# Splitting four elementwise operations of a decoder step into halves: the rotation's multiplication and addition, the low parts of rotated tiles, and the scaling of paired weights

## Chip, cores and metric

The kernel runs on one core of one Trainium2 chip. The metric is the device time of one launch in microseconds; below 3466.3 us stands as the median of three runs of the kernel before (3462.27 to 3474.13). The engines are called as the profile calls them: PE is TensorE, DVE is VectorE, ACT is ScalarE, POOL is GpSimd, SP is SyncE, which here issues all DMAs.

## The reference

One step of a two-layer decoder trunk: a pooling layer, then an attention layer with three dilated groups that share one K/V, for 2048 prompt rows and 8 sample rows of width 1024, all in fp32. What the change touches lies in the projections to q, k and v and in the rotation of q and k:

```python
def rope_partial(x, pos):                     # the first 16 of 64 dims of each head
    half = ROT_DIM // 2
    inv = 1.0 / (ROPE_THETA ** (jnp.arange(0, ROT_DIM, 2, dtype=jnp.float32) / ROT_DIM))
    ang = pos.astype(jnp.float32)[:, None] * inv[None, :]
    cos, sin = jnp.cos(ang)[None, :, None, :], jnp.sin(ang)[None, :, None, :]
    x1, x2 = xr[..., :half], xr[..., half:]
    rot = jnp.concatenate([x1 * cos - x2 * sin, x1 * sin + x2 * cos], axis=-1)
...
kv = (rmsnorm(h, g) @ w_kv).reshape(B, T, N_GROUPS, 2, HEADS_PER_GROUP, HEAD_DIM)
q  = (rmsnorm(h, g) @ w_in)[..., :N_GROUPS * ATTN_WIDTH]      # the rest is the gate
...
y_prompt = rmsnorm(h_p + attn_out(outs_p, gate_p, w_b_out[j]), g_final)
```

The gain `g` of the norm is folded into the weights by the kernel: each weight tile is multiplied by it before use. That is the scaling which the change splits.

## The kernel before, in words

Everything is transposed: 128 features lie on the partitions, tokens along the free axis. Each fp32 matrix is split into a high part (a copy by ACT into the type fp32r) and a low part (the rest, one subtraction), and each product is three matmuls: high by high, high by low, low by high.

The stages, with the time at which each begins in the profiled execution:

1. Pooling layer, from 0 us, in four quarters of 512 tokens.
2. Gates of half 0 (tokens 0 to 1023), from about 657 us.
3. **The paired stage**, from about 757 to 1660 us: q, k and v of half 0. A `Pair` takes the weights of two heads' blocks together (9 for each of 4 head pairs, 36 in all) and makes seven products of half the depth instead of eight (`run_pair`). Its two raw weights of 128x1024 are loaded into `wst` or, for every second pair, `pairh`; `Pair.scale` multiplies each by the gain (`w_scale`, L127, on POOL); `s1` and `s3` (L196, L199, POOL) and `s2` and `s4` (L202, L205, DVE) form sums and differences; `hi` (L212, ACT) and `lo` (L215, DVE) split the seven operands into `ringh` and `ringl`, which PE reads. The results are put together in `raw` (or `pairl`) by ACT copies (L921) and DVE additions (L924).
4. Half 1 (tokens 1024 to 2047), from about 1640 to 3210 us: one weight at a time (`Unit`, whose scaling stays one operation), and beside it, from about 1790 us, the prompt's attention (`prompt_attn`), one step a tick.
5. The output product and the last norm, from about 3220 us.

Rotation (`Rope`): when both heads of a unit are complete, their 16 rotated rows are gathered into one tile `xs` by DMAs (`gather`), three ticks later `turn` multiplies `xs` by the table `cs2` (L790, 128x1024; on DVE in half 0, on POOL in half 1) and adds the lower 64 partitions to the upper 64 (L791, always DVE). DMAs put the rows back into `raw` (L794). Then `split` makes the high part `rh` (L811, ACT) and, two ticks later, `low` subtracts it (L815: DVE in half 0, POOL in half 1) and stores both.

A tick is one `yield` of the dense products, after 8 matmuls or so. `plan` sets at which tick of a product the next weights are loaded, scaled and split; `defer(n, f)` runs f n ticks later. This gives the order in which instructions are written; a scheduler of the framework then fixes the order on each engine's own queue, and from there on each engine works strictly in order. The sample rows' attention (`sample_attn`) runs as a side job in the paired stage, with its products on POOL (L1038, L1070) and its sums on DVE (L1041, L1072).

Of the kernel before, what the change touches and what calls it, by code (L numbers as in the profile page):

```python
# [12 lines left out]
F32 = mybir.dt.float32  # L13
F32R = mybir.dt.float32r
AF = mybir.ActivationFunctionType
OP = mybir.AluOpType
AX = mybir.AxisListType

P = 128
# [4 lines left out]
HALF = 1024  # L24
TOT = SEQ + NB
NQ = 4
QN = SEQ // NQ
# [3 lines left out]
DIL = (1, 4, 16)  # L31
# [22 lines left out]
def step_kernel(ctx: ExitStack, tc: tile.TileContext, a: dict):  # L54
    nc = tc.nc
    vec, act, pool, pe = nc.vector, nc.scalar, nc.gpsimd, nc.tensor
    load_dma = store_dma = nc.sync.dma_start
# [37 lines left out]
    N = type("N", (), {})()  # L95
    N.w1 = rpool

    KH2 = KT // 2
# [27 lines left out]
    def w_scale(st, gs):  # L126
        pool.tensor_tensor(st, st, gs[:, :, None].to_broadcast([P, KT, P]), OP.mult)  # L127
# [19 lines left out]
    class Unit:  # L147
# [9 lines left out]
        def scale(self):  # L157
            if self.gs is not None:
                w_scale(self.st, self.gs)
# [13 lines left out]
    class Pair:  # L173
# [15 lines left out]
                      for i_ in range(2) for j in range(2)}  # L189

        def scale(self, i):
            w_scale(self.st[i], self.gs[i])

        def s1(self):
            self.t = N.bt.tile([P, KH2, P], F32, name="ws1")
# [98 lines left out]
    def defer(ticks, fn):  # L294
        deferred.append([ticks, fn])
# [430 lines left out]
    def perm(ap, g):  # L726

        return ap.rearrange("p (l r) -> p r l", r=DIL[g])

    def permd(ap, g):  # L730
        return ap.rearrange("p (r l) -> p r l", r=DIL[g])
# [36 lines left out]
    class Rope:  # L768
# [18 lines left out]

        def turn(self):
            xs, g, eng = self.xs, self.g, (vec, pool)[self.hf]
            eng.tensor_tensor(permd(xs, g), permd(xs, g), perm(N.cs2, g), OP.mult)  # L790
            vec.tensor_add(xs[0:64], xs[0:64], xs[64:128])  # L791
            for u, (kind, p, raw) in enumerate(self.units):
                for b in range(2):
                    load_dma(raw[64 * b:64 * b + 16], xs[32 * u + 16 * b:32 * u + 16 * b + 16])  # L794
                defer(3 + 2 * u, lambda kind=kind, p=p, raw=raw: self.split(kind, p, raw))

        def dst(self, kind, p, x):
            v = qkd[kind][self.g][p].rearrange("h d x n -> (h d) x n")[:, x]
# [2 lines left out]
        def split(self, kind, p, raw):  # L801
            g = self.g
            if kind == 1:
                if g == 2:
                    store_dma(a["o_k2"][self.hf, p], raw)
                elif self.hf == 1 and g == 0:
                    store_dma(a["o_k0"][p], raw[:, HALF - P:])
                elif self.hf == 1:
                    store_dma(a["o_k1"][p], permd(raw, g)[:, :, P:])
            rh = N.bw.tile([P, HALF], F32R, name="rh", bufs=1)  # L810
            act.activation(rh, raw, AF.Copy)  # L811
            store_dma(self.dst(kind, p, 0), permd(rh.bitcast(F32), g))

            def low():
                (vec, pool)[self.hf].tensor_sub(raw.bitcast(F32R), raw, rh.bitcast(F32))  # L815
                store_dma(self.dst(kind, p, 1), permd(raw, g))
                if self.hf == 1:
                    done[p, g] = done.get((p, g), 0) + 1
            defer(2, low)
# [800 lines left out]
```

## Time and profile before

| | before |
|---|---|
| median of three runs | 3466.3 us (3462.27 to 3474.13) |
| profiled execution, its own time | 3453.65 us |
| span of its instructions | 3451.6 us |
| PE busy | 3187.5 us (92%) |
| DVE busy | 2000.7 us (58%) |
| ACT busy | 1715.3 us (50%) |
| POOL busy | 1680.1 us (49%) |
| mean granted TensorE clock | 0.969 of full speed |

Busy times of engines overlap. PE is busy nearly all the time, so what can be won or lost by the other engines is bounded by how often PE stands still: a look at the waits of PE, stage by stage, comes before a look at what any single instruction takes.

### The profile page before, as it was taken

What the parts mean: (1) busy time and instruction counts of PE and PEld (TensorE: products, weight loads), DVE (VectorE), ACT (ScalarE), POOL (GpSimd) and SP (SyncE); (2) the same over time, 40 slices, a digit from 0 to 9 for tenths busy, and PEclk for the clock granted to TensorE, in tenths of its full rate; (3) what the DMA queues carried; (4) which work ended last, traced back from release to release, by engine and by line L of the source; (5) the groups of instructions that cost most, each with busy time, mean ns of one, the idle gap of its engine ahead of it and who ended that gap; (6) DMA issues with size and microseconds to landing.
All of it is one profiled execution on the core that took longest, in us unless ns stands there. A gap on an engine that the chain in (4) does not pass through costs nothing.

```text
span 3451.6 us, 56978 instructions
## 1 busy us (share of the span) xinstructions
PE 3187.5 (92%) x19608; PEld 2799.4 (81%) x19608; DVE 2000.7 (58%) x3989; ACT 1715.3 (50%) x3812; POOL 1680.1 (49%) x1026
## 2 busy tenths in 40 slices
PE   8999899899998998987989999999999999999798
PEld 8887678699887887877778877888787888887698
DVE  6745665526767667676426555656464646564345
ACT  3333433324434443334227766776666676778221
POOL 5566765624234354343454454545454645552342
PEclk9999999999999999999999999999999999999899
DMA  4434443434576766767777767687777777774653
GB/s 135 145 129 159 141 156 110 129 98 135 154 185 209 177 193 180 201 198 201 195 206 205 194 187 187 189 201 196 181 194 181 198 182 194 196 199 131 192 155 120
DMA packets 547744, 596.96 MB, mean 173 GB/s; under 512 B 216904, under 2 KB 407752, under 8 KB 547448
## 3 DMA queue, kind: packets, MB, share of 16 engines
q1 hardware_dynamic: 547456, 593.32, 61.7%
q8 instruction: 156, 2.56, 0.3%
q14 instruction: 132, 1.08, 0.1%
HBM read 371.77 MB, written 184.04 MB: 161 GB/s over the span
## 4 chain that ended last, share of the span: by engine, by line
PE 32%; DMA 11%; DVE 5%; ACT 4%; SPq 3%; issue 3%; POOL 2%; DVEq 0%; POOLq 0%; ACTq 0%
PE psd L241 20%; PE pss L1211 3%; PE ppt L1232 3%; PE ppo L1276 1%; PE ppo L1278 1%; DMA spb<-pd 1%; DMA statd<-st 1%; ACT pr L1224 1%; DMA vr<-vd 1%; DMA raw<-xs 1%; DMA qt<-qd 1%; DMA wst<-in_wKV 1%; PE ppo L1273 1%; DVE xs L791 1%; DMA cyt<-yd 1%
## 5 line engine op out<-in xcount | busy, mean ns | idle before, releaser
L1163 POOL CAST qt<-qt 64x1024 fp32r<-64x1024 f32 x192 | 207.1, 1079 | 435.1 <-DMA qt<-qd 371.9
L1224 ACT ACTIVATE pr<-pr,st 128x256 f32<-128x256 f32 (+1 forms) x768 | 345.9, 453 | 126.0 <-DVE st L1218 124.7
L1218 DVE CUSTOM_DVE_ANT_0 pr<-pss,mask 128x256 f32<-128x256 f32 (+1 forms) x768 | 248.5, 360 | 175.7 <-PE pss L1211 118.5
L1248 DVE TENSOR_TENSOR pl<-ppt,ph 128x512 fp32r<-128x512 f32 (+2 forms) x384 | 216.1, 570 | 190.0 <-ACT ph L1244 187.2
L168 POOL TENSOR_TENSOR ringl<-wst,ringh 128x1024 fp32r<-128x1024 f32 x96 | 241.6, 2519 | 124.0 <-ACT ringh L163 72.5
L1211 PE MATMUL pss<-kt,qt 128*128 128x256 f32 (+1 forms) x1536 | 261.2, 288 | 12.8 <-DVE st L1218 7.8
L127 POOL TENSOR_TENSOR wst<-wst,gvec 128x1024 f32<-128x1024 f32 x88 | 177.3, 2017 | 184.8 <-DMA wst<-in_wKV 99.1
L241 PE MATMUL psd<-hn_2h,ringh 128*128 128x512 f32 x640 | 259.2, 405 | 6.6 <-ACT raw L837 5.0
L241 PE MATMUL psd<-hn_3h,ringh 128*128 128x512 f32 x640 | 260.9, 408 | 4.1 <-ACT hn_3h L643 2.4
L163 ACT ACTIVATE ringh<-wst 128x1024 fp32r<-128x1024 f32 x184 | 193.3, 1052 | 139.2 <-PE psd L241 94.9
L241 PE MATMUL psd<-hn_2l,ringh 128*128 128x512 f32 x640 | 257.2, 402 | 5.1 <-DVE hn_2l L644 5.1
L241 PE MATMUL psd<-hn_3l,ringh 128*128 128x512 f32 x640 | 259.4, 405 | 2.5 <-DVE hn_3l L644 2.5
L241 PE MATMUL psd<-hn_2h,ringl 128*128 128x512 f32 x640 | 258.7, 404 | 0.0
L241 PE MATMUL psd<-hn_3h,ringl 128*128 128x512 f32 x640 | 258.4, 404 | 0.0
L1211 PEld LDWEIGHTS pss<-kt,qt 128*128 128x128 f32 x1536 | 223.2, 194 | 29.4 <-DVE st L1218 8.7
L1232 PE MATMUL ppt<-ident,pr 128*128 128x128 f32 x1200 | 209.6, 281 | 36.0 <-DVE pl L1248 23.0
L1244 ACT ACTIVATE ph<-ppt 128x512 fp32r<-128x512 f32 (+2 forms) x384 | 189.7, 500 | 91.6 <-PE ppt L1232 87.1
L168 DVE TENSOR_TENSOR ringl<-wst,ringh 128x512 fp32r<-128x512 f32 x176 | 148.4, 878 | 139.5 <-ACT ringh L163 139.3
L970 PE MATMUL pwx<-t1h,ringh 128*128 128x256 f32 (+1 forms) x576 | 171.1, 297 | 26.4 <-DVE pairl L924 14.0
L1232 PEld LDWEIGHTS ppt<-ident,pr 128*128 128x128 f32 x1200 | 143.1, 142 | 63.1 <-issue 22.5
L1190 POOL TENSOR_TENSOR vt<-vr,vt 128x512 fp32r<-128x512 f32 (+1 forms) x96 | 136.4, 1421 | 80.8 <-ACT vt L1189 72.4
L1276 PE MATMUL ppo<-ph,vt 128*128 128x128 f32 (+1 forms) x688 | 167.6, 274 | 7.6 <-ACT ph L1244 5.7
(301 smaller groups left out, 9828.3 us busy)
## 6 DMA issues: line engine op xcount, KB each, us to landing
qt<-qd SPq DMA_DIRECT2D x192, 256.0 KB
wst<-in_wKV SPq DMA_DIRECT2D x72, 512.0 KB
kt<-kd SPq DMA_DIRECT2D x288, 128.0 KB
wst<-in_wA SPq DMA_DIRECT2D x64, 512.0 KB
wst<-in_wQ SPq DMA_DIRECT2D x52, 512.0 KB
kd<-rh SPq DMA_DIRECT2D x48, 512.0 KB
qd<-rh SPq DMA_DIRECT2D x48, 512.0 KB
vd<-vt SPq DMA_DIRECT2D x96, 256.0 KB
```

Source lines behind the costliest of these rows:

```text
L127: pool.tensor_tensor(st, st, gs[:, :, None].to_broadcast([P, KT, P]), OP.mult)
L163: act.activation(self.w[0], self.st, AF.Copy)
L168: self.eng.tensor_sub(self.w[1][:, k], self.st[:, k], self.w[0][:, k].bitcast(F32))
L241: pe.matmul(ps[:, :n], u[:, k, ws], v[:, k, c0:c1], start=(k, i) == order[0], stop=(k, i) == order[-1])
L1163: pool.tensor_copy(qr[64:128], qr[0:64])
L1211: pe.matmul(ps[:, sl], qt[:, x, qc], kt_[:, kc], start=x == 0, stop=x == 1)
L1218: vec.tensor_tensor_reduce(pr[:, lo:], ps[:, sl], mask[:, lo:], 1.0, BIG, OP.add, OP.min, st[:, 0, h, col:col + 1])
L1224: act.activation(pr[:, lo:], pr[:, lo:], AF.Exp, bias=st[:, 0, h, col:col + 1], scale=-1.0, accum_out=st[:, 1, h, col:col + 1])
L1232: pe.transpose(pt[:, (2 * bb + x) * P:(2 * bb + x + 1) * P], pr[:, x * P:(x + 1) * P], ident)
L1244: act.activation(PB[i][0][:, s], pv[:, s], AF.Copy)
L1248: vec.tensor_sub(PB[i][1][:, s], pv[:, s], PB[i][0][:, s].bitcast(F32))
L1276: pe.matmul(po[:, q0:q1], vt[:, kb + 1, h].rearrange("p x d -> p (x d)"), xh, start=first, stop=False, skip_group_check=True)
```

## The change

- `Pair.scale`: 72 multiplications of 128x1024 on POOL become 144 of 128x512.
- `Rope.turn`: the multiplication and the addition are done for one half of the columns, and one tick later (`defer(1, rest)`) for the other; the DMAs back to `raw` and the splits follow that second part. 24 multiplications on DVE, 24 on POOL and 48 additions on DVE become twice as many of half the size.
- `Rope.split`, `low`: in half 0 the 48 subtractions on DVE are done in two halves, the second a tick later, and the store of the low part waits for both. In half 1 nothing changes here.

```diff
--- before.py
+++ after.py
@@ -189,7 +189,10 @@
         def scale(self, i):
-            w_scale(self.st[i], self.gs[i])
+            for j in range(2):
+                k = slice(j * KH2, j * KH2 + KH2)
+                pool.tensor_tensor(self.st[i][:, k], self.st[i][:, k],
+                                   self.gs[i][:, k, None].to_broadcast([P, KH2, P]), OP.mult)
@@ -787,12 +790,22 @@
         def turn(self):
             xs, g, eng = self.xs, self.g, (vec, pool)[self.hf]
-            eng.tensor_tensor(permd(xs, g), permd(xs, g), perm(N.cs2, g), OP.mult)
-            vec.tensor_add(xs[0:64], xs[0:64], xs[64:128])
-            for u, (kind, p, raw) in enumerate(self.units):
-                for b in range(2):
-                    load_dma(raw[64 * b:64 * b + 16], xs[32 * u + 16 * b:32 * u + 16 * b + 16])
-                defer(3 + 2 * u, lambda kind=kind, p=p, raw=raw: self.split(kind, p, raw))
+            lh = HALF // DIL[g] // 2
+
+            def part(i):
+                c = slice(lh * i, lh * i + lh)
+                x = permd(xs, g)[:, :, c]
+                eng.tensor_tensor(x, x, perm(N.cs2, g)[:, :, c], OP.mult)
+                vec.tensor_add(x[0:64], x[0:64], x[64:128])
+            part(0)
+
+            def rest():
+                part(1)
+                for u, (kind, p, raw) in enumerate(self.units):
+                    for b in range(2):
+                        load_dma(raw[64 * b:64 * b + 16], xs[32 * u + 16 * b:32 * u + 16 * b + 16])
+                    defer(3 + 2 * u, lambda kind=kind, p=p, raw=raw: self.split(kind, p, raw))
+            defer(1, rest)
@@ -812,7 +825,18 @@
             def low():
-                (vec, pool)[self.hf].tensor_sub(raw.bitcast(F32R), raw, rh.bitcast(F32))
+                if self.hf == 1:
+                    pool.tensor_sub(raw.bitcast(F32R), raw, rh.bitcast(F32))
+                    fin()
+                else:
+                    lo_part(0)
+                    defer(1, lambda: (lo_part(1), fin()))
+
+            def lo_part(i):
+                c = slice(QN * i, QN * i + QN)
+                vec.tensor_sub(raw[:, c].bitcast(F32R), raw[:, c], rh[:, c].bitcast(F32))
+
+            def fin():
                 store_dma(self.dst(kind, p, 1), permd(raw, g))
```

The queues of the engines stand as follows where the prediction speaks of them. Lines of the changed kernel are its own: L798 and L799 are L790 and L791 of before, L218 is L215, L948 is L924, L205 is L202, L1065 is L1041, L837 is L815 in half 0, L194 is L127 for pairs.

DVE, in the paired stage, at the fourth rotation of the third head pairs (the burst at 1319 us of the profile). Before:

```order
L215 TENSOR_TENSOR ringl<-pairh,ringh 128x512
L790 TENSOR_TENSOR xs<-xs,cs_5539 128x1024
L215 TENSOR_TENSOR ringl<-pairh,ringh 128x512
L791 TENSOR_TENSOR xs<-xs 64x1024
L215 TENSOR_TENSOR ringl<-wst,ringh 128x512
L924 TENSOR_TENSOR pairl<-pairl,pwx 128x256
L202 TENSOR_TENSOR wst<-ws_11746,wst 128x512
L1041 TENSOR_REDUCE sg_t_11720<-skt 35x16
```

The same place in the changed kernel:

```order
L218 TENSOR_TENSOR ringl<-pairh,ringh 128x512
L798 TENSOR_TENSOR xs<-xs,cs_5539 128x4x128 x2
L218 TENSOR_TENSOR ringl<-pairh,ringh 128x512
L799 TENSOR_TENSOR xs<-xs 64x4x128 x2
L218 TENSOR_TENSOR ringl<-wst,ringh 128x512
L948 TENSOR_TENSOR pairl<-pairl,pwx 128x256
L205 TENSOR_TENSOR wst<-ws_11857,wst 128x512
L1065 TENSOR_REDUCE sg_t_11831<-skt 35x16
```

The halves stand where the whole operations stood, both of a kind in a row; nothing else has come between them.

SP, at the end of the attention: the last stores of the merged attention (`yd`, L1366, now L1390) and the first load of an output weight (`in_wB`). Before:

```order
L765 DMA sgd_85<-sgb 128x1024
L1366 DMA yd_93<-ot_31351 128x512
L1499 DMA ch_33346<-h1d_70 128x288
L1458 DMA cyt<-yd_86 128x296
L1366 DMA yd_93<-ot_31600 128x512
L1460 DMA cgt<-sgd_78 128x296
L1499 DMA ch_33346<-h1d_71 128x288
L1458 DMA cyt<-yd_87 128x296
L1458 DMA cyt<-yd_86 128x288
L1460 DMA cgt<-sgd_78 128x288
L123 DMA wst<-in_wB 128x1024
```

In the changed kernel, from the last of these stores but one:

```order
L1390 DMA yd_93<-ot_31586 128x512
L1523 DMA ch_33562<-h1d_71 128x288
L1482 DMA cyt<-yd_87 128x296
L1484 DMA cgt<-sgd_79 128x296
L1523 DMA ch_33562<-h1d_72 128x288
L1390 DMA yd_93<-ot_31826 128x512
L1484 DMA cgt<-sgd_80 128x296
L1482 DMA cyt<-yd_88 128x296
L1523 DMA ch_33562<-h1d_73 128x288
L1482 DMA cyt<-yd_86 128x288
L1484 DMA cgt<-sgd_78 128x288
L123 DMA wst<-in_wB 128x1024
```

Between the last store and the weight there are five DMAs in both; between the last two stores there are now four instead of two.

PE, just ahead of the output product (L1359, now L1383, spreads the merge's weights; the rows with `cy0h` are the first of the output product). Before:

```order
L241 MATMUL psd<-hn_3h,ringl 128x512
L1359 MATMUL pws<-spread_15549,sel 128x512
L241 MATMUL psd<-hn_3h,ringh 128x512
L241 MATMUL psd<-hn_3l,ringh 128x512
L1359 MATMUL pws<-spread_15550,sel 128x512
L241 MATMUL psd<-hn_3h,ringl 128x512
L1359 MATMUL pws<-spread_15550,sel 128x512 x2
L241 MATMUL psd<-cy0h,wbh_33101 128x288
```

In the changed kernel:

```order
L244 MATMUL psd<-hn_3h,ringh 128x512
L244 MATMUL psd<-hn_3l,ringh 128x512
L244 MATMUL psd<-hn_3h,ringl 128x512
L1383 MATMUL pws<-spread_15723,sel 128x512 x3
L1383 MATMUL pws<-spread_15724,sel 128x512 x3
L244 MATMUL psd<-cy0h,wbh_33326 128x288
```

Six of the merge's matmuls now come after the last dense one, where there were two.

## Rows read from the trace of the kernel before

**Rows 1.** The profile's page: span, and busy time of three engines with its share of the span and the number of instructions.
```profile
span 3451.6 us, 56978 instructions
PE 3187.5 (92%) x19608; PEld 2799.4 (81%) x19608; DVE 2000.7 (58%) x3989; ACT 1715.3 (50%) x3812; POOL 1680.1 (49%) x1026
```

**Rows 2.** Busy time of the engines in the paired stage, in half 1 with the attention, and from its end on: stretch, its length, then each engine with its instructions, the granted TensorE clock, the share of DMA engines, GB/s.
```profile
757.00:1660.00 903.00, 813.47 (x5545) 747.41 (x5544) 619.46 (x749) 362.42 (x703) 364.45 (x194) 0.96 0.66 182
1660.00:3180.00 1520.00, 1442.22 (x8831) 1238.38 (x8830) 823.95 (x2415) 1007.08 (x2570) 772.02 (x504) 0.98 0.72 191
3180.00:3452.00 272.00, 232.06 (x1538) 218.67 (x1536) 125.40 (x277) 67.51 (x142) 86.33 (x98) 0.92 0.50 151
```

**Rows 3.** Waits of PE in the paired stage, from 757 to 1660 us: who waited for what, us in total, times, the longest.
```profile
PE pwx L970 <- DVE ringl L215: 22.0, 6, 6.6
PE pwx L970 <- DVE pairl L924: 14.0, 8, 3.2
PE pwx L970 <- DVE raw L924: 10.7, 9, 2.0
PE pwy L970 <- DVE ringl L215: 6.7, 6, 3.2
```

**Rows 4.** Groups of instructions in the paired stage by line and shape, DVE first, then POOL: busy us, mean ns of one, idle time of the engine before them and what ended it.
```profile
L215 DVE TENSOR_TENSOR ringl<-wst,ringh 128x512 fp32r<-128x512 f32 x108 | 104.7, 974 | 40.7 <-ACT ringh L212 20.8 <-PE psd L241 18.5
L215 DVE TENSOR_TENSOR ringl<-pairh,ringh 128x512 fp32r<-128x512 f32 x108 | 101.5, 946 | 20.2 <-ACT ringh L212 18.4
L791 DVE TENSOR_TENSOR xs<-xs 64x1024 f32<-64x1024 f32 x24 | 49.3, 2056 | 0.8
```
```profile
L127 POOL TENSOR_TENSOR wst<-wst,gvec 128x1024 f32<-128x1024 f32 x25 | 54.9, 2201 | 58.5 <-DMA wst<-in_wKV 27.7 <-DVE ringl L215 20.3 <-DVE xs L790 6.3
L127 POOL TENSOR_TENSOR pairh<-pairh,gvec 128x1024 f32<-128x1024 f32 x24 | 51.0, 2138 | 72.1 <-DMA pairh<-in_wKV 64.8 <-DVE ringl L215 7.3
...
L127 POOL TENSOR_TENSOR wst<-wst,gq 128x1024 f32<-128x1024 f32 x13 | 27.0, 2077 | 49.3 <-DVE xs L790 24.5 <-DMA wst<-in_wQ 22.9 <-DVE ringl L215 1.9
...
L127 POOL TENSOR_TENSOR pairh<-pairh,gq 128x1024 f32<-128x1024 f32 x12 | 25.0, 2083 | 64.6 <-DMA pairh<-in_wQ 62.0 <-DVE ringl L215 2.6
```

**Rows 5.** Single durations by line, min/median/max in ns, with the first and the last start in us; the first three in the paired stage, the last two over the whole span.
```profile
L215 DVE TENSOR_TENSOR ringl<-wst,ringh x108: 671/692/2841, 759.3 to 1591.3; 128x512 fp32r<-128x512 f32 x108
```
```profile
L127 POOL TENSOR_TENSOR wst<-wst,gq x13: 1887/1898/2641, 825.0 to 1595.8; 128x1024 f32<-128x1024 f32 x13
```
```profile
L196 POOL TENSOR_TENSOR ws<-wst x18: 1267/1290/1622, 756.3 to 1554.9; 128x512 f32<-128x512 f32 x18
```
```profile
L815 POOL TENSOR_TENSOR raw<-raw,rh x45: 2359/2392/2737, 1687.9 to 3076.8; 128x1024 fp32r<-128x1024 f32 x45
L815 DVE TENSOR_TENSOR raw<-raw,rh x24: 1203/1220/2744, 807.6 to 1657.5; 128x1024 fp32r<-128x1024 f32 x24
```

**Rows 6.** Timeline of the burst at 1319 us: start, duration, engine, line; in brackets the idle time before it and what ended it. DVE, then POOL, then PE.
```profile
1319.12 2.01 DVE L790 TENSOR_TENSOR xs<-xs,cs 128x1024 f32<-128x1024 f32 x1 [2.93 <-DMA sqb<-tokd]
...
1321.76 5.13 DVE L791 TENSOR_TENSOR xs<-xs 64x1024 f32<-64x1024 f32 x1
1327.03 2.17 DVE L215 TENSOR_TENSOR ringl<-wst,ringh 128x512 fp32r<-128x512 f32 x1
```
```profile
1321.07 2.89 POOL L1038 TENSOR_TENSOR skt<-skt,sqb 35x1024 f32<-35x1024 f32 x1 [6.76 <-DMA sqb<-tokd]
1323.92 1.88 POOL L127 TENSOR_TENSOR pairh<-pairh,gq 128x1024 f32<-128x1024 f32 x1
1325.98 2.67 POOL L127 TENSOR_TENSOR pairh<-pairh,gq 128x1024 f32<-128x1024 f32 x1 [0.17 <-DMA pairh<-in_wQ]
```
```profile
1329.25 0.58 PE L970 MATMUL pwx<-hn_0h,ringl 128*128 128x256 f32 x1 [6.62 <-DVE ringl L215]
```

**Rows 7.** Timeline of the burst at 1592 us: DVE, then POOL.
```profile
1592.05 2.92 DVE L791 TENSOR_TENSOR xs<-xs 64x1024 f32<-64x1024 f32 x1
1595.10 0.69 DVE L215 TENSOR_TENSOR ringl<-pairh,ringh 128x512 fp32r<-128x512 f32 x1
```
```profile
1591.99 1.90 POOL L127 TENSOR_TENSOR wst<-wst,gvec 128x1024 f32<-128x1024 f32 x1 [4.01 <-DMA wst<-in_wKV]
```

**Rows 8.** Half 1: the additions of the rotation as a group (1660 to 3180 us), one of them in the timeline, and what POOL does around it; and PE's longest total wait there.
```profile
L791 DVE TENSOR_TENSOR xs<-xs 64x1024 f32<-64x1024 f32 x24 | 47.1, 1961 | 35.7 <-POOL xs L790 21.6 <-DMA qt<-qd 6.1 <-DMA spb<-pd 5.8
```
```profile
2105.43 2.91 DVE L791 TENSOR_TENSOR xs<-xs 64x1024 f32<-64x1024 f32 x1 [4.44 <-POOL xs L790]
```
```profile
2102.50 2.90 POOL L790 TENSOR_TENSOR xs<-xs,cs 128x1024 f32<-128x1024 f32 x1 [0.75 <-DMA xs<-raw]
2105.36 1.90 POOL L127 TENSOR_TENSOR wst<-wst,gq 128x1024 f32<-128x1024 f32 x1
```
```profile
PE ppt L1232 <- DVE pl L1248: 23.0, 15, 4.6
```

**Rows 9.** The end of the attention: timelines of DVE, POOL, SP and PE between 3200 and 3226 us.
```profile
3208.46 2.67 DVE L1361 TENSOR_TENSOR ot<-pws,ot 128x512 f32<-128x512 f32 x4 [4.18 <-PE pws L1359]
```
```profile
3209.30 3.84 POOL L1363 TENSOR_TENSOR ot<-ot,ot 128x512 f32<-128x512 f32 x3 [3.65 <-DVE ot L1361]
```
```profile
3217.26 0.43 SPq L123 DMA_DIRECT2D wst<-in_wB  x1
```
```profile
3223.80 0.58 PE L241 MATMUL psd<-cy0h,wbh 128*128 128x288 f32 x1 [13.40 <-ACT wbh L1441]
```

## The prediction

> **What bounds the kernel now.** I began with the busy times of the page: PE works in 92% of the span, DVE and POOL in 58% and 49% [rows 1]. An operation of DVE or POOL therefore costs something only where PE stands still for it. The table by stages tells how much that can be. In the paired stage PE is busy 813.5 of 903 us, so 89.5 us are idle, at a mean granted clock of 0.96; in half 1 it is 1442 of 1520, 78 idle; at the end 232 of 272, 40 idle [rows 2]. The change touches the first two directly, the third only through the order.
>
> Next come the waits of PE in the paired stage: most of what is named there hangs on DVE, on the low parts L215 (22.0 and 6.7 us) and on the additions L924 (14.0 and 10.7 us in 17 waits) [rows 3]. So DVE is late now and then although it is busy in only 69% of that stage (619 of 903 [rows 2]). The groups say why. L215 takes 0.69 us at its median but 0.97 and 0.95 us in the mean [rows 4, 5]; L791 takes 2.06 us in the mean, where 1.22 us is normal for a DVE operation of as many columns (L815, [rows 5]). Some of these instructions are far longer than their work. The timeline shows when: at 1321.76 L791 takes 5.13 us, across POOL's L1038 and the first L127, and the L215 behind it takes 2.17 us across the second L127 [rows 6]. In [rows 7] L791 begins at 1592.05, just behind a POOL scaling of 1591.99 to 1593.89, and ends at 1594.97, 1.08 us after that scaling. I read this as a turn: a DVE operation with two operands in SBUF stands until the POOL operation ends, then does its work, and POOL's next operation may stand in its turn (the second L127 in [rows 6] takes 2.67 us instead of 1.9).
>
> The price of the turn in the paired stage: over their normal length, the two L215 groups take 104.7 − 108×0.692 = 30 us and 101.5 − 74.7 = 27 us, and L791 49.3 − 24×1.22 = 20 us [rows 4, 5], 77 us together. The scalings are 54.9+51.0+27.0+25.0 = 158 us [rows 4] of POOL's 364 there [rows 2], 43%; an estimate of their share of the hold is thus 33 us.
>
> **The change part by part.**
>
> *Splitting as such.* A DVE operation of 1024 columns takes 1.22 us, two of 512 take 2×0.692 = 1.38: +0.16 us per split [rows 5]. 24 multiplications, 48 additions and 48 subtractions are split on DVE in all its stages: 120×0.16 = 19 us more DVE. The Trainium skill, Perfetto Trace Analysis, section Optimizing Scalar/DVE Operations, gives about 60 ns of overhead per DVE instruction on SBUF; by that the 120 would cost an estimated 7 us, and nothing below would change sign. On POOL a subtraction of 1024 columns takes 2.39 us and a sum of 512 takes 1.29 [rows 5], +0.19; the scaling is quicker (1.90 us at its median [rows 5]), so a half of it is by proportion 1.90×1.29/2.39 = 1.03 us, an estimate, +0.15. For 72 scalings and 24 multiplications that is 15 us more POOL. Both engines have idle time to hold this (31% and 60% in the paired stage). If the cover is gone, as inside a burst, it shows as below.
>
> *Order.* The halves stand where the whole operations stood, in pairs with nothing between them. So the extra tick of `defer` hardly shows in the queues, and the four DMAs of a turn are issued at most a half's length later. The splits (L811) run three ticks or more after, and PE uses the rotated tiles only in half 1: I take 0.
>
> *Bursts with two scalings.* By hand through [rows 6] with halves: POOL's L1038 ends at 1323.96 as before. The change of turn overlaps by some 0.13: L791 ends at 1326.89, 0.91 after the second L127 was begun, and that one is longer by 2.67 − 1.90 = 0.77. So a half scaling costs 1.03 − 0.13 = 0.90 and a half DVE operation 0.69 − 0.13 = 0.56. By turns: half scaling 0.90, half addition 0.56, half scaling 0.90, half addition 0.56, first half of the next scaling 0.90, L215 0.56. Sum 4.38, end 1328.34, against 1327.03+2.17 = 1329.20: −0.8 us of PE's idle 6.62. I find four such bursts (near 1102, 1232, 1319, 1536): −3.2.
>
> *Bursts with one scaling.* [rows 7] with halves: scaling half to 1593.03, addition to 1593.59, scaling half (0.90) to 1594.49, addition to 1595.05, against 1594.97: +0.08, and +0.16 more where the split multiplication ahead delays the first addition. I take +0.2 for each of PE's 17 waits on L924 [rows 3]: +3.4.
>
> *Half 1.* L791 waits here for POOL's multiplication (21.6 us in all) and then averages 1.96 us [rows 8]. In the shown turn POOL multiplies for 2.90 us from 2102.50, and the addition, from 2105.43, is held by the next scaling for 2.91: 5.84 us from begin to end. With halves: multiplication 1.5, addition beside the second multiplication, that one 1.5, then the scaling, one addition held: about 5.9 again. I take 0. Bounds: from −24×(2.91−1.22) = −41 us of DVE time, if no addition is held, to +41 if each is held once more [rows 5, 8]; what reaches PE follows under the rivals.
>
> *The end.* Six of the merge's matmuls instead of two now come after the last dense product, so DVE's L1361 (0.67 each) and POOL's L1363 (1.28 each) [rows 9] end later, by one or two operations of POOL, 1.3 to 2.6 us. Behind them on SP stands the store, and behind that the load of the first output weight, issued at 3217.26, for whose copy PE waits 13.40 us until 3223.80 [rows 9]. I take +2.
>
> Sum: −3.2+3.4+0+2 = **+2 us** on the profiled 3453.65, which itself lies 12.7 below the median of the three runs. Against the median: **3468**.
>
> **The rivals.**
>
> *Faster: the shorter hold reaches PE.* If a held DVE operation on average stands behind half a scaling instead of a whole one, half of the 33 us goes, 16.5. PE then also escapes part of its dips: 903×0.04 = 36 us are lost to the lower granted level in this stage [rows 2], and 16.5/89.5 of that is 6.7. With +2 at the end: 3466.3 − 16.5 − 6.7 + 2 = 3445. If all 33 went, less some 5 for the splits, 3438. For it: the waits on L215, 28.7 us [rows 3], are exactly where the hold is seen. Against it: two halves back to back hold twice, and my walk through [rows 7] gains nothing. The Trainium skill, SBUF — State Buffer, section Who interferes with whom, says that a DVE operation with two SBUF inputs contends with a GpSimd operation that reads SBUF, and that whoever issues first has the port for its whole instruction. By that rule a shorter instruction frees the port sooner; the 5.13 us of [rows 6] agree with it.
>
> *Slower: the second half brings a second hold.* Each turn in half 1 now puts two additions on DVE, each after a POOL operation. If another POOL operation slips in front of each, 24×(2.91−1.22) = 41 us more hold [rows 5, 8]. What waits behind on DVE's queue are the parts of the attention's softmax and `pl`, for which PE already waits 23.0 us [rows 8]. In the paired stage 28.7 of 77 us of hold show up as PE waits on L215, 37%; so here +15. With the +2: 3483; with the splits' own +5 at the upper bound, 3488. It decides as soon as POOL's queue is full during the turn, so that the second addition is held by the scaling just as the first was. For it: POOL follows its multiplication with a scaling at once [rows 8]. Against it: the first addition should find its port free beside a DVE operation's turn.
>
> *The change does nothing.* If the two halves run as one hold, only the splitting is left, and this falls together with my forecast.
>
> **How the numbers follow.** Hand-walked bursts cancel, so no measurable change is likeliest: 0.46 at 3468. The shorter hold has a row that speaks for it: 0.30 at 3445. The double hold: 0.24 at 3483. A difference under 0.3%, 10.4 us, can't be told from none for this kernel; the rivals lie beyond it, so the chances of faster, same and slower are 0.30, 0.46 and 0.24. The range goes from the lower bound of the first rival, 3438, to the upper of the second, 3488; the forecast's own is 3458 to 3477.
>
> **What would show it.** In the profile after, DVE should have 3989+120 = 4109 instructions and POOL 1026+96 = 1122. Scaling halves of 1.1 to 1.2 us in the mean, PE's gap in the two-scaling bursts at 5.8 instead of 6.6, PE's idle time in the paired stage at 89±8, and a gap of 15 to 16 instead of 13.4 before the output product would show my steps right. Idle time under 75 there shows the first rival, and a mean of the half additions in half 1 near 1.9 us each, with longer waits of PE on `pl`, the second. The forecast is wrong if either stage's idle time moves by more than 10 us.

## The result: slower by 1.4%, and the profile after

The changed kernel takes 3515.4 us in the median of six runs (3510.2 to 3523.0), before 3463.4 in the same session; the ratio is 1.0139 with a 95% interval of 1.0123 to 1.0155. Differences below are (ratio − 1) × 3466 us, so this one is **+48 us (43 to 54)**. The forecast of 3468 and its range to 3488 both missed it. (The profiled execution of before lay low, 3453.65; the profiled one of after took 3514.0. The two profiles therefore differ by 60 us and not by 48.)

The page of the changed kernel, which answers to [rows 1]; 4109 instructions on DVE and 1122 on POOL are those that were forecast:

```profile
span 3512.2 us, 57276 instructions
PE 3211.0 (91%) x19608; PEld 2814.7 (80%) x19608; DVE 2060.1 (59%) x4109; ACT 1712.3 (49%) x3812; POOL 1703.4 (48%) x1122
```

Busy time by stage, columns as in [rows 2], cut where PE begins the same products (before: 757, 1658 and 3180):

```profile
761.00:1682.00 921.00, 816.53 (x5535) 749.67 (x5533) 633.94 (x845) 362.80 (x703) 377.46 (x263) 0.95 0.64 178
1682.00:3240.00 1558.00, 1462.21 (x8835) 1251.51 (x8836) 869.11 (x2437) 1003.46 (x2568) 781.09 (x528) 0.97 0.71 186
3240.00:3512.00 272.00, 230.17 (x1542) 217.26 (x1540) 125.28 (x279) 67.97 (x145) 87.14 (x98) 0.92 0.50 151
```

The first two stages of before, with the same cuts:

```profile
757.00:1658.00 901.00, 811.47 (x5536) 745.81 (x5535) 618.77 (x749) 362.27 (x703) 364.35 (x193) 0.96 0.65 182
1658.00:3180.00 1522.00, 1444.22 (x8839) 1239.97 (x8839) 824.64 (x2416) 1007.22 (x2571) 772.13 (x504) 0.98 0.72 191
```

The paired stage takes 921 us instead of 901 and half 1, 1558 instead of 1522; the end is unchanged. In both stages PE's idle time grew, from 89.5 to 104.5 and from 78 to 96, which is more than the 10 us that the prediction named as the sign of being wrong. Its busy time grew too, with the same matmuls at a lower mean granted clock. Waits of PE in the paired stage, as [rows 3]:

```profile
PE pwx L994 <- DVE ringl L218: 28.8, 6, 7.6
PE pwy L994 <- DVE ringl L218: 10.7, 9, 2.3
PE pwx L994 <- DVE raw L948: 9.4, 7, 3.2
PE pwx L994 <- DVE pairl L948: 8.1, 5, 3.2
...
PE pwv L994 <- ACT vt L888: 5.4, 3, 2.6
```

The waits on the low parts in these lines rose from 28.7 to 39.5, and a wait on ACT's `vt` is new. The groups of the stage, as [rows 4] (busy, mean ns of one, idle before):

```profile
L218 DVE TENSOR_TENSOR ringl<-pairh,ringh 128x512 fp32r<-128x512 f32 x108 | 95.1, 886 | 19.1 <-ACT ringh L215 17.2
L218 DVE TENSOR_TENSOR ringl<-wst,ringh 128x512 fp32r<-128x512 f32 x108 | 93.8, 872 | 41.9 <-ACT ringh L215 22.0 <-PE psd L244 18.4
L799 DVE TENSOR_TENSOR xs<-xs 64x512 f32<-64x512 f32 x48 | 57.0, 1187 | 1.6
...
L194 POOL TENSOR_TENSOR pairh<-pairh,gvec 128x512 f32<-128x512 f32 x48 | 60.8, 1292 | 73.7 <-DMA pairh<-in_wKV 73.6
```

The low parts of weights are held less (0.89 and 0.87 us each, before 0.95 and 0.97), as a shorter scaling should give; but the scaling split by itself, below, leaves them at 0.98 and 0.96, and DVE's halves of half 0 by themselves bring them to 0.94 and 0.90: what shortens them goes with DVE's own halves. The additions grow: two halves take 2.37 us together, one whole took 2.06. A half scaling takes 1.29 us in the group shown, where I had expected 1.1 to 1.2.

The burst with two scalings, as [rows 6]: DVE, then POOL, then PE.

```profile
1333.05 2.06 DVE L798 TENSOR_TENSOR xs<-xs,cs 128x512 f32<-128x512 f32 x2 [3.35 <-DMA sqb<-tokd]
1335.03 4.85 DVE L218 TENSOR_TENSOR ringl<-pairh,ringh 128x512 fp32r<-128x512 f32 x1
1339.91 1.41 DVE L799 TENSOR_TENSOR xs<-xs 64x512 f32<-64x512 f32 x2
1341.45 0.69 DVE L218 TENSOR_TENSOR ringl<-wst,ringh 128x512 fp32r<-128x512 f32 x1
```
```profile
1334.97 2.36 POOL L1062 TENSOR_TENSOR skt<-skt,sqb 35x1024 f32<-35x1024 f32 x1 [7.75 <-DMA sqb<-tokd]
1337.30 2.03 POOL L194 TENSOR_TENSOR pairh<-pairh,gq 128x512 f32<-128x512 f32 x2
```
```profile
1342.19 0.58 PE L994 MATMUL pwx<-hn_0h,ringl 128*128 128x256 f32 x1 [6.25 <-DVE ringl L218]
```

PE's gap is 6.25 us, between the 6.62 of before and the 5.8 that I worked out. Here the turn did not pass at all: the low part L218 stood for 4.85 us, until L1062 and both halves of a scaling were through. The gaps of the other three bursts were 2.85, 3.15 and 6.35 us before. Of these the first and the last grew,

```profile
1116.05 0.58 PE L994 MATMUL pwx<-hn_0h,ringl 128*128 128x256 f32 x1 [6.00 <-DVE ringl L218]
```
```profile
1568.10 0.58 PE L994 MATMUL pwx<-hn_0h,ringl 128*128 128x256 f32 x1 [7.55 <-DVE ringl L218]
```

and the second is gone; the four make 19.8 us together instead of 19.0. Two of the kernels below, in which nothing of this stage is changed, have 15.8 (half 1's turn in the old order) and 22.4 (half 1's multiplication alone), so no gain or loss can be read from these gaps.

Half 1, as [rows 8]: the half additions as a group, one turn of them on DVE, and POOL beside it:

```profile
L799 DVE TENSOR_TENSOR xs<-xs 64x512 f32<-64x512 f32 x48 | 79.8, 1662 | 39.3 <-POOL xs L798 27.8 <-DMA kt<-kd 7.1 <-DMA vd<-vt 2.6
```
```profile
1704.51 6.42 DVE L799 TENSOR_TENSOR xs<-xs 64x512 f32<-64x512 f32 x2 [2.35 <-POOL xs L798]
```
```profile
1703.19 2.54 POOL L798 TENSOR_TENSOR xs<-xs,cs 128x512 f32<-128x512 f32 x2 [3.25 <-DMA sqb<-tokd]
1705.68 2.83 POOL L1062 TENSOR_TENSOR skt<-skt,sqb 35x1024 f32<-35x1024 f32 x1
```

The first half addition, ready at 1704.5, stands until POOL's second half multiplication ends at 1705.7, the second until POOL's next two operations have gone: this is the second hold of my slower rival. The 24 turns cost 79.8 us of DVE instead of 47.1. But PE's waits on `pl` did not grow with it; others did. After, then before (cut at 1658 us):

```profile
PE ppt L1256 <- DVE pl L1272: 20.0, 15, 3.0
PE ppo L1300 <- ACT ph L1268: 17.3, 14, 4.0
PE psd L244 <- ACT raw L861: 12.5, 5, 4.1
PE pss L1235 <- DVE st L1242: 10.7, 8, 5.7
```
```profile
PE ppo L1273 <- ACT ph L1244: 9.9, 6, 3.4
...
PE pss L1211 <- DVE st L1218: 7.8, 6, 3.0
PE psd L241 <- ACT raw L837: 6.6, 3, 2.6
PE ppo L1276 <- ACT ph L1244: 5.7, 6, 2.1
```

The first, the longest one of before, fell from 23.0. The second, L1300, is L1276 of before and rose from 5.7; its neighbour L1273, now L1297, fell from 9.9 to 3.6, so that `ppo` waits 20.9 us instead of 15.6. The third, on `psd`, rose from 6.6 to 12.5, the fourth from 7.8 to 10.7. The third points to ACT. The copy of a rotated tile into its high part (`rh`, L811, now L824) stands in ACT's queue among the attention's copies. Its group in half 1 before and after, in the last column the time that ACT sat idle in front of it:

```profile
L811 ACT ACTIVATE rh<-raw 128x1024 fp32r<-128x1024 f32 x45 | 47.5, 1055 | 52.1 <-DMA raw<-xs 38.0 <-DMA kd<-rh 6.1 <-POOL qt L1163 4.2
```
```profile
L824 ACT ACTIVATE rh<-raw 128x1024 fp32r<-128x1024 f32 x45 | 47.4, 1054 | 85.8 <-DMA raw<-xs 69.6 <-POOL qt L1187 9.2 <-POOL pairl L829 5.8
```

One such place in the timeline of ACT, and PE's next matmul:

```profile
2492.65 1.06 ACT L824 ACTIVATE rh<-raw 128x1024 fp32r<-128x1024 f32 x1 [9.21 <-POOL qt L1187]
2493.61 1.02 ACT L861 ACTIVATE raw<-psd 128x512 f32<-128x512 f32 x1
```
```profile
2494.68 0.80 PE L244 MATMUL psd<-hn_3h,ringh 128*128 128x512 f32 x1 [4.12 <-ACT raw L861]
```

ACT stands for 9.2 us in front of the rotated tile, here until POOL's cast of another tile (`qt`) ends; in most of the group's idle time it is the DMA of the rotated rows. Behind it in ACT's queue stands the copy L861, which empties the PSUM tile `psd` that PE waits for.

At the end, as [rows 9], the gap ahead of the output product is 14.40 us instead of 13.40:

```profile
3285.81 0.58 PE L244 MATMUL psd<-cy0h,wbh 128*128 128x288 f32 x1 [14.40 <-ACT wbh L1465]
```

### The profile page after: what moved, and what is told of

Its sections match the earlier page's. It is cut to its first block, busy times and chain, and to the rows that moved or that the text cites. A ratio compares the mean times of both kernels' runs of the same rounds, so it can differ in the third digit from the quotient of the medians.

```text
span 3512.2 us, 57276 instructions
## 1 busy us (share of the span) xinstructions
PE 3211.0 (91%) x19608; PEld 2814.7 (80%) x19608; DVE 2060.1 (59%) x4109; ACT 1712.3 (49%) x3812; POOL 1703.4 (48%) x1122
## 4 chain that ended last, share of the span: by engine, by line
PE 47%; DMA 17%; DVE 14%; SPq 6%; ACT 6%; issue 5%; POOL 4%; DVEq 0%; POOLq 0%; ACTq 0%
PE psd L244 29%; PE pwx L994 4%; PE pss L1235 3%; PE ppt L1256 3%; DVE xs L799 2%; PE pwy L994 2%; DMA xk<-in_xT 2%; DVE sw L538 2%; DMA raw<-xs 1%; SPq L786 1%; PE pwv L994 1%; DVE ringl L218 1%; ACT pr L1248 1%; PE ppo L1300 1%; DMA statd<-st 1%
## 5 line engine op out<-in xcount | busy, mean ns | idle before, releaser
L1235 PE MATMUL pss<-kt,qt 128*128 128x256 f32 (+1 forms) x1536 | 262.2, 289 | 20.1 <-DVE st L1242 10.7
L168 DVE TENSOR_TENSOR ringl<-wst,ringh 128x512 fp32r<-128x512 f32 x176 | 171.3, 1008 | 131.4 <-ACT ringh L163 131.2
L1300 PE MATMUL ppo<-ph,vt 128*128 128x128 f32 (+1 forms) x688 | 171.3, 279 | 21.2 <-ACT ph L1268 17.3
L994 PE MATMUL pwx<-t1h,ringh 128*128 128x256 f32 (+1 forms) x576 | 170.2, 295 | 17.5 <-DVE raw L948 9.4
L127 POOL TENSOR_TENSOR wst<-wst,gvec 128x1024 f32<-128x1024 f32 x64 | 126.4, 1975 | 117.3 <-DMA wst<-in_wKV 54.7
```

Of the source, the lines that this page charges most:

```text
L168: self.eng.tensor_sub(self.w[1][:, k], self.st[:, k], self.w[0][:, k].bitcast(F32))
L994: pe.matmul(ps[:, :c1 - c0], u[:, k], v[:, k, c0:c1], start=(first and k == 0 and j == 0), stop=(k == KH2 - 1 and j == 2), skip_group_chec ...
L1235: pe.matmul(ps[:, sl], qt[:, x, qc], kt_[:, kc], start=x == 0, stop=x == 1)
L1300: pe.matmul(po[:, q0:q1], vt[:, kb + 1, h].rearrange("p x d -> p (x d)"), xh, start=first, stop=False, skip_group_check=True)
```

## Experiments

**One part at a time, in the order that the scheduler lays.** Each takes over the hunk of the change that its name says, and is compared with runs of the kernel before beside it, as are all kernels below; the two turns are chosen by `if self.hf == 1:` and `if self.hf == 0:` around the new and the old body.

> Only the turn of half 1 is split (multiplication on POOL, addition on DVE, the second part one tick later); half 0 and the scaling are as before. Theory A (a second hold: POOL's second half multiplication starts at once, so the first half addition on DVE stands until it ends, the second behind POOL's next operation, and the softmax's DVE work queues behind): most of the loss of half 1, +28 to +38 us, that is 3492 to 3502; the half additions average 1.8 us or more in half 1. Rival B (half 0's halves are what costs, half 1 only inherits work that lies later): within 8 us of before. Rival C (the tick of delay makes the rotated tiles late for the attention): also +28 to +38, but with half additions near 0.7 to 1.2 us.

> Only the turn of half 0 is split (both operations on DVE). Theory A: two DVE halves back to back are held twice by whatever POOL runs, and in bursts L215 comes later: +5 to +12 us, 3469 to 3476. Rival D (the costs of the paired stage come from the split scaling, which offers POOL twice as many turns): 0 to +3. Rival E (each part alone is harmless, only together they fill the bursts): within 3 us.

> Only the subtraction of the low parts in half 0 is split on DVE, its store waits for both. Theory A: 48 more pieces that can each be held, in front of L215: +3 to +8 us, 3466 to 3472. Rivals D and E: within 3 us.

> Only the scaling of paired weights is split on POOL. Theory A: a whole DVE operation stands behind a half scaling at most, and POOL pays the turn: -8 to 0 us, 3455 to 3463, with L215's means below 0.9 us. Rival D: +8 to +15 us, since POOL gets in twice as often. Rival E: within 3 us.

Measured: half 1's turn +36 us (26 to 47), half 0's turn +44 (34 to 55), low parts +16 (11 to 21), scaling +3 (−4 to 10). The first hit theory A's +28 to +38, with additions of 1.66 us where it had asked for 1.8; the same halves in the old order, below, show that this was luck. The scaling alone left the low parts' means at 0.97 and 0.90 us, not below 0.9. The four add up to twice the change's +48, so they can't be four separate costs. Half 0's turn also lost some 23 us in half 1 by its profile, where its code is that of before. What all but the scaling have in common is the order: in the kernel with the scaling split the attention's products lie where they lay against the dense ones, in the other three some 90% of its matmuls of scores (L1211) have moved, by 8 to 12 dense matmuls in the mean. The framework's scheduler lays the queues by its own model of the durations, so another length on DVE can move the whole attention. That gave the next theory: the order costs, not the halves.

**Halves and order apart.** A table of issue order holds every engine's queue to a recorded one; it adds no wait:

```diff
+            for x, y in zip(seq, seq[1:]):
+                tc.add_manual_dep(own[y], own[x].name, mybir.DependencyInfo(
+                    mybir.DependencyClass.NoSync, mybir.DependencyReason.DATA), reason="pinned")
```

In the first kernel the halves stand in the place of their wholes (`rest()` in place of `defer(1, rest)`, and the same for the low parts), in the second the wholes in the place of their halves (`defer(4, self.turn)` for `defer(3, self.turn)`), the third does that, without the later tick, for the order of the kernel with half 0's turn split, the fourth has the tick alone and no table.

> All four operations in halves as in the change, but the second half issued at once and every engine's queue held to the order of the kernel before, each pair of halves in the place of its whole. Theory A (the halves cost: a second hold on DVE): most of the loss stays, 3500 to 3515, with half additions of 1.8 us or more in the mean in half 1. Theory F (the order costs: the framework's scheduler lays the attention and the dense products differently against each other for any change of DVE's or POOL's work, and half 1 loses by that): within 10 us of before, 3458 to 3478. If both hold, in between: about 3485 to 3495.

> The counterpart: nothing is split, the turn of the rotation comes one tick later, and every engine's queue is held to the order of the changed kernel, the whole operation in the place of its last half. Theory F: most of the loss is there without any half, 3500 to 3515. Theory A: within 10 us of before.

> The kernel before, nothing split, but every queue held to the order of the kernel in which half 0's turn alone was split (that one took 3512, although half 1's code was that of before). Theory F: 3495 to 3512, with the loss in half 1 and in the paired stage as there. Theory A: within 10 us of before in the paired stage, so at most 3490, by the 23 us that half 1 lost there.

> The kernel before with the whole turn one tick later, order as the scheduler lays it. Theory C (the tick makes the rotated tiles late): +10 us or more. Theory F: anything between -10 and +30, since this is another order again; theory A: within 8 us.

Measured: **halves in the old order +15 us (9 to 22); nothing split in the new order +34 (22 to 45)**; nothing split in the order of half 0's turn +26 (16 to 37); one tick alone +5 (−1 to 10). 1.0044 × 1.0097 is 1.0141, the change's 1.0139. So both theories hold in part, and the order is the larger one. ACT's group `rh` in half 1 and PE's waits of the kernel with the new order and nothing split:

```profile
L811 ACT ACTIVATE rh<-raw 128x1024 fp32r<-128x1024 f32 x45 | 47.4, 1054 | 95.8 <-DMA raw<-xs 79.5 <-issue 9.3 <-POOL pairl L815 6.1
```
```profile
PE psd L241 <- ACT raw L837: 14.4, 6, 5.0
PE pss L1211 <- DVE st L1218: 14.2, 7, 6.7
PE pst L1047 <- DVE sg_t L1041: 8.7, 2, 7.9
```

and ACT's group in the kernel with halves in the old order:

```profile
L824 ACT ACTIVATE rh<-raw 128x1024 fp32r<-128x1024 f32 x45 | 47.5, 1055 | 62.7 <-DMA raw<-xs 44.5 <-DMA kd<-rh 6.5 <-POOL qt L1188 4.6
```

The waits that grew in half 1 of the changed kernel grow with the order alone, and ACT's 85.8 us belong to it too. PE's waits on the low parts in the paired stage do not: 32.8 us in the kernel with the new order and nothing split, 43.1 with halves in the old order.

**Which halves cost, in the old order.** The hunks as in the first study, without ticks, under the table; the last splits half 1's multiplication and leaves its addition whole.

> Of the halves at the old order (all four together: +17 us) only those of half 1's turn, multiplication on POOL and addition on DVE, every queue as before. Theory A (second hold in half 1): +8 to +15 us, 3475 to 3483, the two half additions of a turn together 3.0 us or more against 1.96 of the whole one. Rival G (the halves of half 0 cost, in front of L215): 0 to +4.

> Only the DVE halves of half 0 at the old order: its turn and its low parts. Theory A: +4 to +8 us, as each piece costs 0.16 us and can be held of its own, with PE's waits on ringl up by about as much. Rival G: +12 to +17.

> Only the paired scalings in halves, at the old order. Theory A: DVE stands shorter behind POOL, -6 to +2 us. Rival D (more turns for POOL): +5 to +12.

> At the old order, only half 1's multiplication on POOL in two halves; the addition stays whole and so comes behind both. Theory A (it is the first half addition, caught behind POOL's second multiplication, that costs): within 3 us of before. Rival H (POOL's own longer work, 0.19 us a turn, or its longer chain to the addition): as much as the kernel with both halves.

Measured: half 1's turn +5 us (−2 to 12), half 0's DVE operations **+22** (18 to 27), the scaling **−8** (−13 to −3), half 1's multiplication alone −1 (−6 to 3). Together 19, against the 15 of all four. The second hold of half 1 is there in the first of them too, 73.6 us of additions instead of 47.1,

```profile
L797 DVE TENSOR_TENSOR xs<-xs 64x512 f32<-64x512 f32 x48 | 73.6, 1533 | 23.0 <-POOL xs L796 14.0 <-DMA kt<-kd 3.9 <-DMA wst<-in_wQ 2.2
```

and yet it costs no more than 12 us: the +28 to +38 of theory A are out, the +8 to +15 that it still gave for this kernel only in part. In half 0 PE's waits on the low parts rise to 45.2 us; with this stage unchanged they are 28.7 (before), 27.9 (half 1's turn) and 34.9 (half 1's multiplication):

```profile
PE pwx L1000 <- DVE ringl L215: 33.4, 8, 7.2
...
PE pwy L1000 <- DVE ringl L215: 11.8, 12, 3.1
```

The split scaling in the old order is the only version that beats both kernels, at 0.9976 (0.9962 to 0.9991); in its own order, with a few matmuls elsewhere, the same split gained nothing (+3, −4 to 10). Its trace does not show the low parts held less or PE waiting less for them, so by what way it gains is open; the additions of the rotation take 41.5 us instead of 49.3, and PE's waits on the additions L924 (here L927) fell from 24.7 to 19.6:

```profile
L218 DVE TENSOR_TENSOR ringl<-pairh,ringh 128x512 fp32r<-128x512 f32 x108 | 105.6, 984 | 18.2 <-ACT ringh L215 16.6
L218 DVE TENSOR_TENSOR ringl<-wst,ringh 128x512 fp32r<-128x512 f32 x108 | 103.5, 963 | 42.3 <-ACT ringh L215 22.8 <-PE psd L244 18.4
```
```profile
PE pwx L973 <- DVE ringl L218: 20.9, 9, 6.3
PE pwy L973 <- DVE ringl L218: 16.2, 16, 1.9
```

With the runs of the next study the order of each part can be priced, as the loss in its own order less the loss in the old one: half 1's turn 31 us, half 0's turn 22 (26 when measured with nothing split), the low parts 5. The order of the kernel with the low parts split moved the scores the furthest of the three, by 12 dense matmuls in the mean, and costs the least: how far the attention has moved does not tell what it costs.

**What of half 0, and which queue.** The turn alone, the low parts alone, short copies in place of any split (below, three times), and all halves with a table for PE alone.

```diff
+            if self.hf == 0:
+                vec.tensor_copy(N.pad, ones[:, 0:16])
```

> At the old order, only half 0's turn in halves on DVE (48 more instructions). If the turn, which stands right in front of L215 in the bursts, carries the loss of half 0's DVE halves (+22 us): +12 to +20. If both share it by number: +9 to +13. If the low parts carry it: 0 to +6.

> At the old order, only half 0's low parts in halves on DVE (48 more instructions, the store waits for both). The counterpart of the turn alone: +3 to +8 if the turn carries the loss, +9 to +13 if both share it, +15 to +22 if the low parts do.

> Nothing is split; behind each multiplication, addition and low part of half 0 DVE has one more short copy of 128x16 with a single operand in SBUF (96 of them, about 0.16 us each, 15 us of DVE), which computes nothing that is used; order as before. If the halves cost by DVE's own extra time and instruction count in front of L215: +12 to +22 us. If they cost by a second hold behind POOL: 0 to +8.

> All four operations in halves, issued at once; only PE's queue is held to the order of the kernel before, the scheduler lays the other four. If the loss by the order (+36 us) is one of PE's queue: as with all five queues held, +12 to +22 us. If it is one of DVE's, ACT's or SP's: +30 or more.

Measured: turn +22 us (16 to 28), low parts +11 (7 to 15), which is more than the +22 of both, so the two don't add up; short copies +15 (9 to 20); PE's queue alone held +14 (9 to 20), as with all five held. Holding PE's queue is thus enough. It does not part PE's order from ACT's, which follows: ACT's instructions then stand in the places of before for 91% again, in the changed kernel for 57%. The copies did not separate what they were made to separate, for they were held as well:

```profile
L797 DVE COPY pad<-ones 128x16 f32<-128x16 f32 x24 | 24.1, 1005 | 0.8
L823 DVE COPY pad<-ones 128x16 f32<-128x16 f32 x48 | 14.6, 303 | 0.0
L794 DVE COPY pad<-ones 128x16 f32<-128x16 f32 x24 | 8.1, 338 | 0.0
```

They took 47 us for the 16 that their medians, 0.17 to 0.18 us, would make; 16 of the 96 took over a microsecond. That 96 more short DVE instructions in these places cost about 15 us is shown; whether by their own length or by the hold is not. PE's waits on the low parts, 33.1 us in this trace, do not show where: they lie within what the stage has unchanged.

**Where the order costs.** The order of half 0's turn (+26 us with nothing split), for PE's queue alone, cut at the end of the paired stage; the other part in the old order.

> Nothing split; PE's queue up to the end of the paired stage in the order of the kernel with half 0's turn split, from there on in the order of before, the other queues as the scheduler lays them. If the order costs in half 1, where the attention lies against the dense products: 0 to +6 us. If it costs in the paired stage, as that kernel's profile with +27 us there says: +15 to +26.

> The counterpart: PE's queue as before up to the end of the paired stage, then as in the kernel with half 0's turn split. If the order costs in half 1: +15 to +26 us. If in the paired stage: 0 to +10.

Measured: +8 us (2 to 14) and +6 (0 to 12). Neither part reaches the +15 that a single place should have given. Their sum, 14, is below 26, though the intervals allow for both; no run holds PE's queue alone to the whole new order, so a share of the other four queues, which these two left to the scheduler, is not excluded. Where in the queue the 34 us of the change's own order arise stays open beyond the waits shown above.

## Why the prediction was wrong, step by step

- **"Order … I take 0" failed, by 34 us.** It looked at DVE's pairs of halves and at the four DMAs, and not at PE's queue, in which the attention had moved through all of half 1. The rows on PE's queue ahead of the prediction show its end alone, where matmuls had moved; ACT's 52.1 us of idle time in front of `rh` in the profile of before is the sort of wait that a moved attention brings out. No rival held it either: the one that had the direction right, slower, had it for the second hold in half 1, which costs at most 12 us.
- **"Both engines have idle time to hold this" failed, by some 20 us.** I charged the 96 splits of half 0 only in bursts (+3.4, on PE's waits for the additions L924, which fell from 24.7 to 17.5). Measured in the old order they are +22 (18 to 27). The cover was an average: DVE idles 31% of the stage, but its turns and low parts stand in front of `ringl`, for which PE was already waiting 28.7 us [rows 3] and waits 45.2 with these halves. Whether a piece costs by its length or by being held again is not shown.
- **Bursts with two scalings, −3.2.** The gap walked through fell by 0.4 and not 0.8, since there the turn did not pass between POOL's operations. I took it four times, though the other three bursts differ; the four together went from 19.0 to 19.8 us, within what they vary by with the stage unchanged. The scaling by itself, in the old order, gained 8 us (3 to 13), a third of the 23 that the first rival had it gain. The sign that this rival named, PE's idle time in the stage under 75 us, is not in its trace (87.5), nor is there less waiting on the low parts, so its mechanism is not shown.
- **Half 1, 0.** In the old order +5 (−2 to 12): the step holds within its uncertainty, its reason doesn't. I took the first addition to run beside the second multiplication; it is held by it. Of the 41 us more of DVE time that the slower rival named, 33 came about, 26.5 in the old order. The 37% that I let reach PE would make 10 of these, which the measurement neither shows nor excludes; the waits on `pl`, where they should have shown, fell.
- **The end, +2.** The gap grew by 1.0 us, half of what I took. It goes with the order: 15.6 us with the new order and nothing split, 13.1 to 13.6 in all kernels with the five queues held to the old one.
- **Sum.** 34 (order) + 22 (half 0 on DVE) − 8 (scaling) + 5 (half 1) = 53, or 49 with the 15 of all halves measured together, against 48 (43 to 54) measured.

The Trainium skill, Perfetto Trace Analysis, section Optimizing Scalar/DVE Operations, says of ScalarE and VectorE that breaking up their instructions may let work finish sooner where they are not saturated but make other engines wait. The runs do not agree for DVE's operations of half 0: in that stage DVE is 69% busy and PE waits for it, and splitting them cost 22 us.

## What to carry to other kernels

Where a scheduler lays the queues by modelled durations, a change of an instruction's length can be a change of order too, on the engine that bounds the kernel first of all; compare that engine's queue before pricing the edit, and hold the order fixed to measure the edit itself. That the order moved does not say what it costs: here other orders cost from about 5 to 34 us. Splitting the instruction that others stand behind gained a little (the scaling, 8 us); splitting the one that stands gave it a second time to stand (the additions of half 1, 73.6 us instead of 47.1). An engine that idles a third of the time need not cover anything if its queue stands just in front of what the bounding engine waits for.

## What the runs showed of the hardware that I had not expected

- A short DVE copy with a single operand in SBUF (128x16, 0.17 to 0.18 us at its median) was held behind POOL, once for 5.90 us across three POOL operations, in the timeline of DVE in the kernel with them:

```profile
1107.99 5.90 DVE L797 COPY pad<-ones 128x16 f32<-128x16 f32 x1
```

The Trainium skill, SBUF — State Buffer, section Who interferes with whom, counts `copy` among the operations that can take the port shared with GpSimd; the trace agrees.
- Of 58 times that a DVE operation stood when one half scaling followed another at once, it came in between them 55 times by my count in the changed kernel's trace; but behind POOL's operation on 35 partitions (L1062, 35x1024) it failed to do so 4 times of 8, and then stood for one more POOL operation (three times) or two (once, in the burst shown).
